# Gate products of the recurrent layers: plain fp32 matmuls replaced by three fp32r passes, and modulation vectors moved between layers

## The chip, the cores and the metric

The kernel runs on one core of one Trainium2 chip, as one launch. The metric is device time in microseconds (us); the profile shows one execution of the same program with a record for every instruction. Five engines matter here: PE (TensorE) multiplies matrices, PEld is the part of PE's queue that loads the stationary operand, DVE (VectorE) and ACT (ScalarE) work on tiles element by element, and SP only issues DMA transfers.

## The reference

One inference step runs two token streams, 128 context tokens and 256 latent tokens (384 columns in the kernel), through four layers of width 1024: a recurrent layer (RG-LRU), a Conformer convolution layer, a neighbourhood-attention layer, and a second recurrent layer. Each layer is a mixer and then an MLP with a squared ReLU, both behind a normalisation that is modulated by six vectors computed from the conditioning (shift, scale and gate for the mixer, and again for the MLP).

```python
h = _modulate(x, sh1, sc1)                       # rmsnorm(x) * (1 + sc1) + sh1
gate_br, rec = jnp.split(h @ w_in, 2, axis=-1)
xf = _dwconv_centred(rec, conv_w, conv_b)        # 4 taps along time
# both directions, blocks of 256 channels:
r  = jax.nn.sigmoid(_block_diag(xf, w_a, b_a))
ig = jax.nn.sigmoid(_block_diag(xf, w_x, b_x))
log_a = -LRU_C * r * jax.nn.softplus(-lam)
a = jnp.exp(log_a)
bx = jnp.sqrt(-jnp.expm1(2.0 * log_a)) * (ig * xf)
h_t = a_t * h_(t-1) + bx_t                       # linear scan
y = (hs_f + hs_b) * gelu(gate_br)
return y @ w_out
```

The products `_block_diag` are the gate products that the change touches. Everything is in fp32.

## The kernel before

**Layout.** Channels lie on the 128 partitions, tokens on the free axis, so a width of 1024 is eight tiles of 128x384. A weight chunk is 128x2048 fp32 (1 MB): two output tiles of eight 128x128 blocks each, or, for the gates, the sixteen 128x128 blocks of one 256-channel block (two directions, two gates, two output tiles, two inputs).

**fp32r with splits.** PE takes fp32r operands, a shorter form of fp32. To keep the precision, the kernel splits each operand into a high and a low part: ACT copies it to an fp32r tile (the high part), and DVE subtracts that from the original (the low part). `mm3` (L452) then issues three matmuls into one PSUM tile: high weight with high input, high weight with low input, low weight with high input. Weights are split when loaded, in `load_chunk` (L196): one DMA into `raw` (two buffers), then for each half an ACT copy at L210 into `whi` and a DVE subtraction at L211 into `wlo` (five buffers each, of half a chunk).

**The gates do otherwise.** A gates chunk is loaded as two 512 KB pieces into `graw` tiles of the layer's own pool (three buffers, L197 to L202), isn't split, and `gates` (L593) multiplies the fp32 tile `xf` with it directly (L605): sixteen fp32 matmuls of 386 columns in each call. The profile shows each of these as two records.

**A recurrent layer** (`lru`, L561) goes through four blocks `b` of 256 channels. `rec(b)` makes the recurrent input, and `conv` (L572) turns it on DVE into `xf` (one multiplication at L584 and three at L587 for each of two tiles). `gates(b)` multiplies, and then ACT computes tanh (L606), exp and tanh (L611, L613), a square (L617) and a square root (L620), while DVE multiplies (L618, L619, L621), scans in both directions (L627, L629), saves the states (L631, L632) and adds the directions (L633). `gbr(b)` computes the gelu branch (L641 to L645), `combine(b)` (L654) multiplies both, and `outs(b)` splits the result (L388, L389) into `yh` and `yl` for the output product `lout`. The tiles `tr` of the gates have two buffers, `ti` and `a` have one, and PSUM tiles for products have six.

**Order.** The order of the calls at the end of `lru` (L715 to L746) and the plan of chunks (`weight_plan`) set the order of the weights; `chunk` (L221) loads one chunk ahead. A scheduler of the language places the instructions of each engine by this order and by when it believes their inputs ready, so a later instruction can stand in front of an earlier one that waits. At run time each engine takes its instructions in the order so fixed. SP issues the weight loads and the modulation loads from one queue.

**Modulation vectors.** There are 192 (four layers, six vectors, eight tiles), made in a fixed order. `pe_mod` makes some on PE; `dve_mod` (L310) makes one on DVE from a 512 KB load, with two multiply-and-accumulate instructions over 1024 columns (L323) and a small addition (L326). `mods(n, pe)` in `lru` does `n` of the one and `pe` of the other in the first layer; the tables `MLPMODS`, `ATTMODS` and the number `VALMODS` (L93 to L98) say how many `dve_mod` follow each step of the MLPs and of the attention layer, and `need` makes those that are still missing.

Of the kernel before, what the change touches and what calls it, by code (L numbers as in the profile page):

```python
# [7 lines left out]
F32 = mybir.dt.float32  # L8
F32R = mybir.dt.float32r
# [5 lines left out]
P = 128  # L15
# [45 lines left out]
def weight_plan():  # L61
    plan = []
    for l in range(DEPTH):
# [11 lines left out]
        for half in range(2):  # L75
# [14 lines left out]
WARM0, WARM1, WARM2 = 20, 8, 4  # L90
RECLAG, PRE1 = 2, 8
WARM3 = (6, 6)
MLPMODS = {(False, 0, 1): (0, 1, 2, 1, 2, 1, 2, 1), (False, 0, 2): (2, 2, 2, 1, 2, 2, 2, 1),  # L93
           (False, 1, 1): (2, 2, 2, 1, 2, 2, 2, 1), (False, 1, 2): (0, 0, 0, 0, 0, 0, 0, 0),
           (True, 0, 1): (0, 1, 1, 1, 1, 2, 2, 0), (True, 0, 2): (0,) * 8,
           (True, 1, 1): (0,) * 8, (True, 1, 2): (0,) * 8}
ATTMODS = (0, 1, 1, 1, 1, 1, 1, 1)
VALMODS = 0  # L98
PTB, BTB = 3, 3
NMOD = DEPTH * 6 * KT  # L100
MODS = []
# [12 lines left out]
def trunk(ctx, tc, wst, wmod, vecs, condr, xin, kcT, vcache, rpbt, diag, ident_in,  # L114
# [33 lines left out]
    def mod_load(i, pool=None, into=None):  # L148
        at = i
        if into is not None:  # L150
            w = into
        elif at < 2 or at in (12, 13) or at > 15:
            w = wp.tile([P, D], F32, tag="pmw", name=f"pmw{i}", bufs=2)
        elif at < 5 or at > 13:
            w = wp.tile([P, D], F32, tag="dmw", name=f"pmw{i}", bufs=3)
        elif at < 9:
            tg, nb = (("tr", 2), ("ti", 1), ("a", 1), ("tr", 2))[at - 5]
            w = pool.tile([P, 4 * LG], F32, tag=tg, name=f"pmw{i}", bufs=nb)[:, :D]
        else:
            w = pool.tile([P, D], F32, tag="graw", name=f"pmw{i}", bufs=3)  # L160
        nc.sync.dma_start(w, wmod[i])
        return w

# [30 lines left out]
    loaded = {}  # L194

    def load_chunk(i):  # L196
        if plan[i][0] == "gates":  # L197
            g = []
            for d in range(2):
                g.append(state["lp"].tile([P, 1024], F32, tag="graw", name=f"graw{i}{d}", bufs=3))  # L200
                nc.sync.dma_start(g[d], wst[i, :, d * 1024:d * 1024 + 1024])
            return g  # L202
        raw = wp.tile([P, 2048], F32, tag="raw", name=f"raw{i}", bufs=2)
        nc.sync.dma_start(raw, wst[i])
        his, los = [], []
        for h in range(2):
            s = slice(h * 1024, h * 1024 + 1024)
            hi = wp.tile([P, 1024], F32R, tag="whi", name=f"whi{i}_{h}", bufs=5)
            lo = wp.tile([P, 1024], F32R, tag="wlo", name=f"wlo{i}_{h}", bufs=5)
            nc.scalar.activation(hi, raw[:, s], AF.Copy)  # L210
            nc.vector.tensor_tensor(lo, raw[:, s], hi.bitcast(F32), op=ALU.subtract)  # L211
            his.append(hi)
            los.append(lo)
        return his, los
# [346 lines left out]
    def lru(l, j, nrm):  # L561
        with tc.tile_pool(name=f"lru{l}", bufs=1) as lp:
# [4 lines left out]
                nc.gpsimd.memset(r, 0.0)  # L567
                recs.append(r)
            nst = lp.tile([P, 2, KT], F32, name=f"nst{l}")
            xfs, gls = {}, {}  # L570

            def conv(b, i, ps, c=None):  # L572
                t = 2 * b + i
                r = recs[t % 2]
                for s, xa, xb in SEG:
                    o = 1 + 2 * s
                    if c is None:
                        nc.scalar.activation(r[:, xa + o:xb + o], ps[:, xa:xb], AF.Copy)
                    else:
                        nc.scalar.activation(r[:, xa + o:xb + o], ps[:, xa:xb], AF.Identity, bias=c[:, s:s + 1])  # L580
                if b not in xfs:
                    xfs[b] = lp.tile([P, 2, LG], F32, tag="xf", name=f"xf{l}{b}", bufs=2)
                xf = xfs[b][:, i]
                nc.vector.tensor_scalar(xf, r[:, 0:LG], lcw[:, j, t, 0:1], lcb[:, j, t:t + 1],  # L584
                                        op0=ALU.mult, op1=ALU.add)
                for k in range(1, 4):
                    nc.vector.scalar_tensor_tensor(xf, r[:, k:k + LG], lcw[:, j, t, k:k + 1], xf,  # L587
                                                   op0=ALU.mult, op1=ALU.add)

            def rec(b):  # L590
                lin([chunk("rec", j, b)], h, f"rec{l}_{b}_", lambda i, ps: conv(b, i, ps))

            def gates(b):  # L593
                cs = chunk("gates", j, b)
                tr = lp.tile([P, 4, LG], F32, tag="tr", name=f"tr{l}{b}", bufs=2)
                ti = lp.tile([P, 4, LG], F32, tag="ti", name=f"ti{l}{b}")
                a = lp.tile([P, 4, LG], F32, tag="a", name=f"a{l}{b}")
# [1 line left out]
                for d in range(2):  # L599
                    for wh in range(2):  # L600
                        for mt in range(2):
                            ps = mm_tile(f"g{l}{b}{d}{wh}{mt}")[:, :LG]
                            for k in range(2):
                                o = ((wh * 2 + mt) * 2 + k) * P
                                matmul(ps, cs[d][:, o:o + P], xf[:, k], start=k == 0, stop=k == 1)  # L605
                            nc.scalar.activation((tr if wh == 0 else ti)[:, d * 2 + mt], ps, AF.Tanh, scale=0.5,  # L606
                                                 bias=hba_[:, wh, j, d, 2 * b + mt:2 * b + mt + 1])
                    for mt in range(2):
                        t = 2 * b + mt
                        i = d * 2 + mt  # L610
                        nc.scalar.activation(a[:, i], tr[:, i], AF.Exp, scale=nch[:, j, d, t:t + 1],  # L611
                                             bias=nch[:, j, d, t:t + 1])
                        nc.scalar.activation(tr[:, i], tr[:, i], AF.Tanh, scale=ch[:, j, d, t:t + 1],  # L613
                                             bias=ch[:, j, d, t:t + 1])
                    s = slice(2 * d, 2 * d + 2)
                    q = lp.tile([P, 2, LG], F32, tag="q", name=f"q{l}{b}{d}")
                    nc.scalar.activation(q, a[:, s], AF.Square)  # L617
                    nc.vector.scalar_tensor_tensor(tr[:, s], q, 1.0, tr[:, s], op0=ALU.add, op1=ALU.mult)  # L618
                    nc.vector.scalar_tensor_tensor(ti[:, s], ti[:, s], 1.0, xf, op0=ALU.add, op1=ALU.mult)  # L619
# [34 lines left out]
                    nc.vector.tensor_tensor(gl[:, :, xa:xb], hs[:, 0:2, a:e_], gl[:, :, xa:xb], op=ALU.mult)  # L654

            def outs(b):
                if b < 3:
                    w_ = lp.tile([P, 1024], F32R, tag="graw", name=f"yh{l}{b}", bufs=3)
                else:
                    w_ = lp.tile([P, 4 * LG], F32R, tag="a", name=f"yh{l}{b}")  # L660
                if b:
# [54 lines left out]
            mods(1)  # L716
            q = gates(0)
            combine(0, q)
            mods(2, 2)
            rec(2)  # L720
            mods(0, 2)
            q1 = gates(1)
            mods(2, 2)
            rec(3)
            mods(0, 2)
            q2 = gates(2)
            mods(2, 2)
            gbr(1)
            mods(0, 2)
            combine(1, q1)  # L730
            q3 = gates(3)
            outs(0)
            outs(1)
            mods(1, 2)
            gbr(2)
            mods(0, 2)
            combine(2, q2)
# [8 lines left out]
            return out_proj(l, "lout", j, y, f"lo{l}")  # L746

    def mlp(l, nrm):
        last = l == DEPTH - 1
        with tc.tile_pool(name=f"mlp{l}", bufs=1) as mp:  # L750
            for half in range(2):
                hid = []
# [17 lines left out]
                while i < 8:  # L770
# [3 lines left out]
                    else:  # L774
                        lin([chunk("ff1", l, half * 8 + i)], h, f"f{l}{half}{i}_", act_)
                        i += 1
                    dve_mod(MLPMODS[last, half, 1][i - 1])
                mv = need(l, G2)
                if half == 1:
                    nx = Norm(l + 1, SC1, SH1)  # L780
                for m in range(KT):
# [5 lines left out]
                    residual(m, ps, G2, mv)  # L787
                    if half == 1:
                        nx.add(m)
                    dve_mod(MLPMODS[last, half, 2][m])  # L790
        return nx

    hb1 = cst.tile([P, 2 * KT], F32, name="hb1")
# [560 lines left out]
```

## Time and profile before

| | us |
|---|---|
| median of 3 runs (1773.96 to 1775.02) | 1774.39 |
| the profiled execution, first to last instruction (its span) | 1769.4 |
| ... of it PE busy | 1741.5 |
| ... DVE busy | 1388.3 |
| ... ACT busy | 939.8 |
| first recurrent mixer, from the first convolution to the last split output | 44 to 168 |
| second recurrent mixer, from the first normalised tile to the last split output | 1349 to 1468 |

The profiled execution has no other time than its span; the median of the runs is 5.0 us longer than that span, which is what lies around the first and the last instruction. The windows of the last two rows are those in which the gates are computed. A window of the profile gives, for each engine, the time in which it had an instruction at work.

### The profile page before, as it was taken

How to read it: one execution, taken by the hardware profiler on the slowest of the kernel's cores; microseconds unless marked ns; L12 is line 12 of the kernel's file. 1: busy time of each engine (PE TensorE's matmuls, PEld its weight loads, DVE VectorE, ACT ScalarE, POOL GpSimd, SP SyncE). 2: the span in 40 equal slices, each digit the busy share in tenths (PEclk: the TensorE clock that was granted, in tenths of full speed). 3: DMA queues.
4: the chain of work that ended last, by engine and by line, in shares of the span. 5: the costliest groups of instructions: out<-in, count | busy, mean ns of one | idle time of the engine just before them, and what ended most of it. 6: DMA issues, size and time to landing. Idle time of an engine off the chain costs nothing.

```text
span 1769.4 us, 27427 instructions
## 1 busy us (share of the span) xinstructions
PE 1741.5 (98%) x10524; PEld 1638.2 (93%) x10524; DVE 1388.3 (78%) x2759; ACT 939.8 (53%) x1691; POOL 21.6 (1%) x46
## 2 busy tenths in 40 slices
PE   8999999999999999999999999999999999999997
PEld 7778999999985999999987889999999789999997
DVE  5998889895697889888576788998997878853443
ACT  4876662453533774254365556624545976733531
POOL 0000000000021000000000000000000000000000
PEclk9999999999999999999999999999999999999999
DMA  9666367663386247765345533676663413543341
GB/s 388 231 215 222 127 222 250 237 248 135 120 240 188 80 151 258 240 242 205 123 171 183 165 112 130 236 250 228 244 242 120 136 67 120 197 148 119 119 135 45
DMA packets 66996, 322.43 MB, mean 182 GB/s; under 512 B 7952, under 2 KB 12176, under 8 KB 43696
## 3 DMA queue, kind: packets, MB, share of 16 engines
q1 hardware_dynamic: 64944, 314.11, 51.5%
q0 software_dynamic: 1920, 6.57, 1.6%
q8 instruction: 82, 1.34, 0.3%
q14 instruction: 50, 0.41, 0.1%
HBM read 316.69 MB, written 3.96 MB: 181 GB/s over the span
## 4 chain that ended last, share of the span: by engine, by line
PE 84%; DVE 8%; ACT 4%; DMA 3%; issue 1%; SPq 0%; POOL 0%; DVEq 0%; ACTq 0%
PE f L125 30%; PE o L125 30%; PE pw L125 4%; PE qk L125 4%; PE lo L125 3%; PE p L125 2%; PE wo L125 2%; PE v L125 2%; PE rec L125 1%; DMA pmw<-wmod 1%; PE cps L125 1%; DVE wlo L211 1%; PE gbr L125 1%; PE po L125 1%; DVE xf L587 1%
## 5 line engine op out<-in xcount | busy, mean ns | idle before, releaser
L210 ACT ACTIVATE whi<-raw 128x1024 fp32r<-128x1024 f32 x360 | 378.0, 1058 | 557.8 <-PE o L125 337.8
L211 DVE TENSOR_TENSOR wlo<-raw,whi 128x1024 fp32r<-128x1024 f32 x360 | 437.8, 1220 | 166.5 <-ACT whi L210 166.4
L323 DVE SCALAR_TENSOR_TENSOR mjunk<-dmw,condb 128x1024 bf16<-128x1024 f32 x300 | 365.2, 1217 | 1.3
L125 PE MATMUL o<-hl,whi 128*128 128x384 f32 x1024 | 343.0, 335 | 0.0
L125 PE MATMUL o<-hh,wlo 128*128 128x384 f32 x1024 | 343.0, 335 | 0.0
L125 PE MATMUL o<-hh,whi 128*128 128x384 f32 x1024 | 343.0, 335 | 0.0
L125 PEld LDWEIGHTS o<-hh,wlo 128*128 128x128 f32 x1024 | 192.2, 188 | 0.0
L125 PEld LDWEIGHTS o<-hh,whi 128*128 128x128 f32 x1024 | 192.2, 188 | 0.0
L125 PEld LDWEIGHTS o<-hl,whi 128*128 128x128 f32 x1024 | 192.2, 188 | 0.0
L480 DVE SCALAR_TENSOR_TENSOR x<-o,modv,x 128x128 f32<-128x128 f32 (+1 forms) x128 | 47.4, 412 | 87.8 <-PE o L125 87.6
L125 PE MATMUL g<-xf,graw 128*128 128x386 f32 x256 | 87.3, 497 | 1.9 <-DVE gl L645 1.9
L125 PEld LDWEIGHTS g<-xf,graw 128*128 128x128 f32 x256 | 48.7, 192 | 35.4 <-DVE gl L645 2.6
L766 DVE TENSOR_TENSOR hl<-s,hh 128x384 fp32r<-128x384 f32 x128 | 70.9, 554 | 13.4 <-ACT s L765 8.7
L764 ACT ACTIVATE hh<-r 128x384 fp32r<-128x384 f32 x128 | 67.1, 524 | 3.5
L765 ACT ACTIVATE s<-r 128x384 f32<-128x384 f32 x128 | 65.1, 509 | 0.0
L760 ACT ACTIVATE r<-f 128x384 f32<-128x384 f32 x112 | 53.2, 475 | 7.8 <-PE f L125 7.8
L125 PE MATMUL lo<-yh,wlo 128*128 128x384 f32 x128 | 43.3, 338 | 0.1
L125 PE MATMUL lo<-yh,whi 128*128 128x384 f32 x128 | 43.3, 340 | 0.0
L125 PE MATMUL lo<-yl,whi 128*128 128x384 f32 x128 | 43.0, 336 | 0.0
L125 PE MATMUL cps<-z,dg 128*32 128x399 f32 (+2 forms) x448 | 34.7, 468 | 3.9 <-DMA z<-zd 3.9
L876 DVE SCALAR_TENSOR_TENSOR zt<-zp,vec,zt 128x399 f32<-128x399 f32 x58 | 36.7, 632 | 1.2
L125 PEld LDWEIGHTS cps<-z,dg 128*32 128x32 f32 x448 | 15.1, 114 | 22.7 <-issue 21.5
(1510 smaller groups left out, 4041.2 us busy)
## 6 DMA issues: line engine op xcount, KB each, us to landing
raw<-wst SPq DMA_DIRECT2D x180, 1024.0 KB, 5.0
dmw<-wmod SPq DMA_DIRECT2D x150, 512.0 KB, 4.2
pmw<-wmod SPq DMA_DIRECT2D x38, 512.0 KB, 6.5
graw<-wst SPq DMA_DIRECT2D x16, 512.0 KB, 5.6
bt<-rpbt SPq DMA_DIRECT2D x16, 384.0 KB, 3.8
z<-zd POOLq DMA_DIRECT2D x24, 213.5 KB, 6.5
dg<-diag SPq DMA_DIRECT2D x6, 512.0 KB, 4.2
pmwl<-wmod SPq DMA_DIRECT2D x4, 512.0 KB, 6.8
```

The source lines that it names most:

```text
L125: i = nc.tensor.matmul(*a, **kw)
L210: nc.scalar.activation(hi, raw[:, s], AF.Copy)
L211: nc.vector.tensor_tensor(lo, raw[:, s], hi.bitcast(F32), op=ALU.subtract)
L323: nc.vector.scalar_tensor_tensor(mjunk, w, 0.5, condb[:, s], op0=ALU.mult, op1=ALU.mult, accum_out=mod_tile(l)[:, c, m, s:s + 1]))
L480: nc.vector.scalar_tensor_tensor(x[m][:, xa:xb], ps[:, a:b], mv[:, g, m, s:s + 1], x[m][:, xa:xb], op0=ALU.mult, op1=ALU.add)
L587: nc.vector.scalar_tensor_tensor(xf, r[:, k:k + LG], lcw[:, j, t, k:k + 1], xf, op0=ALU.mult, op1=ALU.add)
L760: nc.scalar.activation(r, ps[:, :N], AF.Relu)
L764: nc.scalar.activation(hh, r, AF.Square)
L765: nc.scalar.activation(s, r, AF.Square)
L766: nc.vector.tensor_tensor(hl, s, hh.bitcast(F32), op=ALU.subtract)
L876: nc.vector.scalar_tensor_tensor(t, z[:, k:k + CG], dww[:, m, k:k + 1], t, op0=ALU.mult, op1=ALU.add)
```

## The change

- `load_chunk` loses its branch for the gates. A gates chunk is now loaded like any other: one 1 MB DMA into `raw`, two ACT copies into `whi`, two DVE subtractions into `wlo`.
- `conv` splits each `xf` tile as soon as it is made, into `xh` (ACT) and `xl` (DVE), new tiles with two buffers each. `xf` itself stays, since L619 reads it.
- `gates` issues `mm3` in place of one fp32 matmul: 48 fp32r matmuls of 386 columns in each call in place of 16 fp32 ones.
- The pool `graw` is gone. The `yh` tiles of `outs` for b = 0, 1, 2 now lie in `xh`, `xh` and `xl`, and the loads of modulation vectors 9, 10 and 11 go to buffers of `whi`, `wlo` and `dmw`.
- The numbers of `dve_mod` change. By the calls, four leave the mixer of the first layer (three of `mods(2, 2)` become `mods(1, 2)`, one `mods(1, 2)` becomes `mods(0, 2)`; the short title says six). Two of them go to the first half of the first MLP, two to the start of the attention layer (`VALMODS`), and the attention's last step makes one that `need` made there before. `MLPMODS` now has an entry for each layer.

```diff
-MLPMODS = {(False, 0, 1): (0, 1, 2, 1, 2, 1, 2, 1), (False, 0, 2): (2, 2, 2, 1, 2, 2, 2, 1),
...
-ATTMODS = (0, 1, 1, 1, 1, 1, 1, 1)
-VALMODS = 0
+MLPMODS = [((0, 1, 2, 1, 2, 2, 2, 2), (2, 2, 2, 1, 2, 2, 2, 1), (2, 2, 2, 1, 2, 2, 2, 1), (0,) * 8),
+           ((0, 1, 2, 1, 2, 1, 2, 1), (2, 2, 2, 1, 2, 2, 2, 1), (2, 2, 2, 1, 2, 2, 2, 1), (0,) * 8),
...
+ATTMODS = (0, 1, 1, 1, 1, 1, 1, 2)
+VALMODS = 2
...
-            w = pool.tile([P, D], F32, tag="graw", name=f"pmw{i}", bufs=3)
+            tg, nb = (("whi", 5), ("wlo", 5), ("dmw", 3))[at - 9]
+            w = wp.tile([P, D], F32, tag=tg, name=f"pmw{i}", bufs=nb)
...
-        if plan[i][0] == "gates":
-            g = []
-            for d in range(2):
-                g.append(state["lp"].tile([P, 1024], F32, tag="graw", name=f"graw{i}{d}", bufs=3))
-                nc.sync.dma_start(g[d], wst[i, :, d * 1024:d * 1024 + 1024])
-            return g
...
+                    xss[b] = (lp.tile([P, 2, LG], F32R, tag="xh", name=f"xh{l}{b}", bufs=2),
+                              lp.tile([P, 2, LG], F32R, tag="xl", name=f"xl{l}{b}", bufs=2))
...
+                split(xf, xss[b][0][:, i], xss[b][1][:, i])
...
-                cs = chunk("gates", j, b)
+                whs, wls = chunk("gates", j, b)
+                xh, xl = xss[b]
...
-                                matmul(ps, cs[d][:, o:o + P], xf[:, k], start=k == 0, stop=k == 1)
+                                mm3(ps, whs[d][:, o:o + P], wls[d][:, o:o + P], (xh[:, k], xl[:, k]), k == 0, k == 1)
...
-                if b < 3:
-                    w_ = lp.tile([P, 1024], F32R, tag="graw", name=f"yh{l}{b}", bufs=3)
+                if b < 2:
+                    w_ = lp.tile([P, 2 * LG], F32R, tag="xh", name=f"yh{l}{b}", bufs=2)
+                elif b == 2:
+                    w_ = lp.tile([P, 2 * LG], F32R, tag="xl", name=f"yh{l}{b}", bufs=2)
...
-            mods(2, 2)
+            mods(1, 2)
             rec(2)
             mods(0, 2)
             q1 = gates(1)
-            mods(2, 2)
+            mods(1, 2)
             rec(3)
             mods(0, 2)
             q2 = gates(2)
-            mods(2, 2)
+            mods(1, 2)
             gbr(1)
...
             outs(1)
-            mods(1, 2)
+            mods(0, 2)
             gbr(2)
...
-                    dve_mod(MLPMODS[last, half, 1][i - 1])
+                    dve_mod(MLPMODS[l][2 * half][i - 1])
```

More of the change, by code (lines that the diff above doesn't have):

```diff
@@ L92 @@
 WARM3 = (6, 6)
-MLPMODS = {(False, 0, 1): (0, 1, 2, 1, 2, 1, 2, 1), (False, 0, 2): (2, 2, 2, 1, 2, 2, 2, 1),
-           (False, 1, 1): (2, 2, 2, 1, 2, 2, 2, 1), (False, 1, 2): (0, 0, 0, 0, 0, 0, 0, 0),
-           (True, 0, 1): (0, 1, 1, 1, 1, 2, 2, 0), (True, 0, 2): (0,) * 8,
-           (True, 1, 1): (0,) * 8, (True, 1, 2): (0,) * 8}
-ATTMODS = (0, 1, 1, 1, 1, 1, 1, 1)
-VALMODS = 0
+MLPMODS = [((0, 1, 2, 1, 2, 2, 2, 2), (2, 2, 2, 1, 2, 2, 2, 1), (2, 2, 2, 1, 2, 2, 2, 1), (0,) * 8),
+           ((0, 1, 2, 1, 2, 1, 2, 1), (2, 2, 2, 1, 2, 2, 2, 1), (2, 2, 2, 1, 2, 2, 2, 1), (0,) * 8),
+           ((0, 1, 2, 1, 2, 1, 2, 1), (2, 2, 2, 1, 2, 2, 2, 1), (2, 2, 2, 1, 2, 2, 2, 1), (0,) * 8),
+           ((0, 1, 1, 1, 1, 2, 2, 0), (0,) * 8, (0,) * 8, (0,) * 8)]
+ATTMODS = (0, 1, 1, 1, 1, 1, 1, 2)
+VALMODS = 2
 PTB, BTB = 3, 3
@@ L569, in lru @@
             nst = lp.tile([P, 2, KT], F32, name=f"nst{l}")
-            xfs, gls = {}, {}
+            xfs, xss, gls = {}, {}, {}
             def conv(b, i, ps, c=None):
@@ L748, in mlp @@
     def mlp(l, nrm):
-        last = l == DEPTH - 1
         with tc.tile_pool(name=f"mlp{l}", bufs=1) as mp:
@@ L789, in mlp @@
                         nx.add(m)
-                    dve_mod(MLPMODS[last, half, 2][m])
+                    dve_mod(MLPMODS[l][2 * half + 1][m])
         return nx
```

## The prediction

> **What bounds the kernel now.** I read first the page's head, then its chain that ended last.
>
> ```profile
> span 1769.4 us, 27427 instructions
> PE 1741.5 (98%) x10524; PEld 1638.2 (93%) x10524; DVE 1388.3 (78%) x2759; ACT 939.8 (53%) x1691; POOL 21.6 (1%) x46
> PE 84%; DVE 8%; ACT 4%; DMA 3%; issue 1%; SPq 0%; POOL 0%; DVEq 0%; ACTq 0%
> ```
>
> PE fills 98% of the span, so whatever shortens PE's work seems to shorten the kernel. But shares are averages over stages, and the change touches only the two recurrent mixers. So next I asked for the busy time by windows: the two mixers from the first convolution to the last split output, then one turn of each (from the start of one block's gates to the start of the next block's).
>
> ```profile
> core 0: us, PE busy (x) PEld busy (x) DVE busy (x) ACT busy (x) POOL busy (x), PEclk, DMA share, GB/s
> 44.00:168.00 124.00, 121.47 (x836) 97.89 (x835) 115.58 (x231) 94.01 (x161) 0.00 (x0) 1.00 0.65 224
> 1349.00:1468.00 119.00, 116.97 (x548) 98.08 (x547) 101.91 (x184) 95.75 (x158) 0.00 (x0) 0.99 0.29 93
> 78.81:100.48 21.67, 21.67 (x152) 16.33 (x148) 21.67 (x39) 18.08 (x29) 0.00 (x0) 1.00 0.68 210
> 1385.69:1404.47 18.78, 18.78 (x81) 14.47 (x81) 17.23 (x29) 17.30 (x28) 0.00 (x0) 1.00 0.33 112
> ```
>
> Here PE isn't alone. In the first mixer DVE works 115.58 of 124 us and is idle 8.4; in its turn both engines are full. In the second DVE is idle 17.1 of 119, and in its turn PE is full with DVE and ACT at 92%. Any gain of PE has to pass two engines with little room, and the change gives both more to do.
>
> The end of the window matters, since there PE waits for y:
>
> ```profile
> 1466.20 1.03 DVE L389 TENSOR_TENSOR yl<-gl,yh 128x384 fp32r<-128x384 f32 x2 [0.59 <-ACT yh L388]
> 1467.10 0.34 PE L125 MATMUL lo<-yl,whi 128*128 128x384 f32 x1
> ```
>
> DVE ends the last split at 1467.2 and PE reads a low part at 1467.1, in the same us. If DVE ends later, PE stands still; if PE comes earlier, it waits. So the mixer's time is that of the later of the two.
>
> **PE's part.** The price of a gates call and of 48 fp32r passes, from the timeline of PE:
>
> ```profile
> 1358.55 0.34 PE L125 MATMUL gbr<-h310h,whi 128*128 128x384 f32 x1
> 1366.93 0.49 PE L125 MATMUL g<-xf,graw 128*128 128x386 f32 x1
> 1385.69 10.56 PE L125 MATMUL g<-xf,graw 128*128 128x386 f32 x32
> 1395.79 0.64 PE L125 MATMUL rec<-h310h,whi 128*128 128x384 f32 x1
> ```
>
> The 48 passes of a gbr chunk take 1366.93 - 1358.55 = 8.38 us. A gates call (32 records) and the 48 passes behind it take the turn's 18.78; with two calls of 48 passes it would be 16.76. That is 2.0 us less for each call, 16 us for eight. If PE alone set the pace, the span would fall by 16.
>
> A rule of the Trainium skill ("Perfetto Trace Analysis", section Identifying the Most-Contended Engine) judges PE by the busy time of its weight loads, not of its matmuls. The loads' records here are 188 ns, so 48 passes would need 9.0 us by it and the gain would be 11 us instead of 16; the measured 8.38 decides, and the forecast below uses neither.
>
> **DVE's and ACT's part.** The operations that are added have rows of their own kind:
>
> ```profile
> L210 ACT ACTIVATE whi<-raw 128x1024 fp32r<-128x1024 f32 x360 | 378.0, 1058 | 557.8 <-PE o L125 337.8
> L211 DVE TENSOR_TENSOR wlo<-raw,whi 128x1024 fp32r<-128x1024 f32 x360 | 437.8, 1220 | 166.5 <-ACT whi L210 166.4
> L323 DVE SCALAR_TENSOR_TENSOR mjunk<-dmw,condb 128x1024 bf16<-128x1024 f32 x300 | 365.2, 1217 | 1.3
> ...
> L388 ACT ACTIVATE yh<-gl 128x384 fp32r<-128x384 f32 x8 | 3.8, 521 | 6.7 <-DVE gl L654 6.7
> 1372.16 2.35 DVE L211 TENSOR_TENSOR wlo<-raw,whi 128x1024 fp32r<-128x1024 f32 x2
> 160.14 1.02 DVE L389 TENSOR_TENSOR yl<-gl,yh 128x384 fp32r<-128x384 f32 x2
> ```
>
> Back to back, two weight subtractions take 2.35 us, so one more costs DVE 1.14 (their ends overlap); two 384-column subtractions take 1.02, so one more costs 0.47. Each mixer gets eight of the first (four gates chunks, two halves) and eight of the second (four blocks, two tiles): 9.1 + 3.8 = 12.9 us of DVE. ACT gets eight copies of at most 1.05 and eight of at most 0.52: 12.6 us.
>
> In the first mixer four modulation vectors leave. One is two instructions of group L323: 365.2 / 150 = 2.43 us, so 9.7 us of DVE go. Net, DVE gets 12.9 - 9.7 = 3.2 us in the first mixer and 12.9 in the second, where there is nothing to take out: 16.1 us together. By turns: in the second mixer DVE comes to 17.23 + 2 x 1.14 + 2 x 0.47 = 20.5 and ACT to 17.30 + 3.1 = 20.4, against PE's 16.8 and the 18.78 that a turn takes today. In the first, DVE comes to 21.67 + 3.2 - 2.4 = 22.5 against PE's 19.7 and today's 21.67. Both mixers become DVE's, and both turns longer.
>
> How much longer depends on how much of DVE's idle time the added work fills. That time, 8.4 + 17.1 = 25.5 us, is waiting for ACT:
>
> ```profile
> DVE tr L618 <- ACT q L617: 7.8, 4, 4.3
> DVE ti L621 <- ACT tr L620: 6.4, 4, 1.7
> ...
> ACT a L611 <- DVE nst L631: 2.7, 2, 1.4
> ACT ti L606 <- DVE nst L631: 2.6, 1, 2.6
> ACT tr L606 <- DVE gl L654: 2.9, 1, 2.9
> ...
> PE g L125 <- DVE gl L645: 1.9, 1, 1.9
> ```
>
> (All of the second mixer.) DVE waits for ACT's square and square root of the same block, while ACT waits for DVE's scans to free `a`, `ti` and `tr`; weight splits can stand in the first kind of gap, but no split shortens the chain. So some idle time stays. I take 8.4 us for each mixer: that is what the first mixer keeps today with DVE and PE both nearly full. Then the first takes 115.58 + 3.2 + 8.4 = 127.2 (+3.2) and the second 101.91 + 12.9 + 8.4 = 123.2 (+4.2): **+7.4 us**. Bounds: idle time filled to nothing gives 16.1 - 25.5 = -9.4; none of it filled gives +16.1.
>
> **The small edits.** The four vectors land in the first MLP and in the attention layer:
>
> ```profile
> 200.00:330.00 130.00, 130.00 (x748) 130.00 (x747) 119.32 (x222) 61.75 (x100) 0.00 (x0) 1.00 0.65 219
> 900.00:945.00 45.00, 45.00 (x223) 34.75 (x223) 31.31 (x81) 27.16 (x52) 0.00 (x0) 1.00 0.42 147
> ```
> ```profile
> PE pmp L125 <- DMA pmw<-wmod: 0.3, 1, 0.3
> ```
>
> Each place gets two, 4.9 us of DVE, into 10.7 and 13.7 us of DVE's idle time with PE full, and two loads of 512 KB, where the DMA engines are busy 0.65 and 0.42 of the time: nothing. Without that cover it would be up to 4.9 in the first place. Gates chunks now pass `raw` and its two buffers: the same bytes, and DVE's subtraction must be done before SP can issue the load two chunks on, with the modulation loads queued behind it; PE waited 0.3 us in all for those loads in the first mixer (the last row), so I take 0, with up to 2. The first pass of a gates call now waits for one more copy and one more subtraction behind the last tap of the convolution, 0.52 + 0.55 us (1.02 less 0.47); where PE has just been fed, that is hidden behind the 8.38 us of the product in front of it, and where DVE is late it is in the sum above. A copy L210 for a gates chunk stands in ACT's queue and waits for a weight buffer; behind it stand the tanhs (L606) that empty PSUM for PE: part of the ACT coupling, and of the upper bound. Vectors 9 to 11 and `yh` only change buffers: 0; the first gbr chunk must now wait for a buffer of the first rec chunk, at most one copy and one subtraction, 2.3 us.
>
> **Sum.** Against the profiled execution 1769.4 + 7.4 = 1776.8; the median is 5.0 us above that span, so 1774.4 + 7.4 = 1781.8. A measurement of this kernel can tell about 0.2% (3.5 us) from no change.
>
> **Rivals.**
> 1. *The idle time is filled (faster).* With DVE behind, its queue always holds a ready split, and PE runs ahead with later products. All 25.5 us filled give 1774.4 - 9.4 = 1765.0. It decides once DVE keeps less than 25.5 - 16.1 = 9.4 us idle in both mixers. For it: the turn of the first mixer shows no idle time at all. Against: the block chain above. Chance 0.14.
> 2. *The full gain of PE arrives,* 1774.4 - 16 = 1758.4. DVE's work would have to leave the windows: 118.8 and 114.8 us don't fit into 116 and 111. Chance 0.07.
> 3. *Fill and load balance.* Idle time falls to about 9.4, the kernel stays within 3.5 us of 1774.4; also where the change wouldn't do what it says, three passes costing what fp32 costs. Chance 0.23.
> 4. *Nothing is filled,* since ACT (94.01 and 95.75 plus 12.6) is as tight as DVE: 1774.4 + 16.1 = 1790.5. It decides if the second mixer's 17.1 us of idle time stays. Chance 0.12.
> 5. *The clock falls.* PE will wait in each turn. One such wait is in the trace:
>
> ```profile
> 1423.23:1437.23 14.00, 12.05 (x33) 6.60 (x33) 12.07 (x19) 7.64 (x13) 0.00 (x0) 0.88 0.23 75
> ```
>
> Behind the 1.9 us wait the granted clock of 14 us is 0.88, 1.7 us lost. In each of eight calls, and on the chain, that is 13.4 us on top of the forecast: 1795. Mostly it would hide, as PE has 3 us of room in a turn. The Trainium skill ("TensorE: Matmul & The Clock Gate", Part 1) has the clock at half after an idle window of about 3.4 us; the trace shows a fall after less. Chance 0.04.
>
> **How the numbers follow.** The forecast itself (+3.5 to +12) has 0.40. Slower by over 0.2%: 0.40 + 0.12 + 0.04 = 0.56; same 0.23; faster 0.14 + 0.07 = 0.21. The likeliest case's own range is 1778 to 1786. The range reaches from the filled case less 1 to the unfilled case plus the small edits' 2: 1764 to 1792.
>
> **What would show it.** Right: in the windows from the first `xf` to the last `yl`, DVE busy about 119 and 115 us with around 8 idle, PE busy falling to some 113 and 109 with waits "PE g <- DVE" or PE waiting for `xl`; the second mixer's turn 20.5 or more; g in x48 passes with some 8.4 us from first to last where nothing stops it; MLPs and attention unchanged. Wrong: a turn of the second mixer under 18.8, DVE idle under 9 us in both mixers together, or a change of over 3 us outside the two mixers.

## The result, and the profile after

The changed kernel takes 1783.38 us (median of 4 runs, 1781.84 to 1785.01) against 1774.70 for the kernel before beside it (4 runs): a ratio of 1.0051, 95% interval 1.0038 to 1.0065. It is slower by 8.7 us; the forecast was 1781.8. (The times below are medians of 4 to 12 executions, that of before_again is a single one; one of the ten of copies_back took 6991 us and is not in its ratio.)

The head of the page after has almost the same shares as before:

```profile
span 1780.1 us, 27727 instructions
PE 1736.6 (98%) x10652; PEld 1667.0 (94%) x10652; DVE 1413.0 (79%) x2793; ACT 961.7 (54%) x1723; POOL 21.6 (1%) x46
```

PE's busy time fell by 4.9 us where sixteen were to be saved, and DVE's rose by 24.7. The profiled execution took 1780.1 us, 10.7 more than that of before. A run's time is only 1.7 us above its span (this one counts as 1781.84), so the 5.0 us between median and span of before, which the prediction took for what lies around the execution, were mostly scatter between executions. The profile of before was some 3 us quicker than its kernel's median, and this one 1.5; so the stages below add up to more than the 8.7 us between the medians.

Where did the 10.7 us come from? The first product of each normalisation is a border between two stages. From the timeline of PE, before and then after:

```profile
196.54 0.81 PE L125 MATMUL n_4p<-n_4a,ones 128*128 128x384 f32 x2
465.20 0.81 PE L125 MATMUL n_1p<-n_1a,ones 128*128 128x384 f32 x2
620.33 0.81 PE L125 MATMUL n_4p<-n_4a,ones 128*128 128x384 f32 x2
888.99 0.81 PE L125 MATMUL n_1p<-n_1a,ones 128*128 128x384 f32 x2
1075.80 0.81 PE L125 MATMUL n_4p<-n_4a,ones 128*128 128x384 f32 x2
1344.46 0.81 PE L125 MATMUL n_1p<-n_1a,ones 128*128 128x384 f32 x2
1492.56 0.81 PE L125 MATMUL n_4p<-n_4a,ones 128*128 128x384 f32 x2
```
```profile
202.34 0.81 PE L125 MATMUL n_4p<-n_4a,ones 128*128 128x384 f32 x2
470.99 0.81 PE L125 MATMUL n_1p<-n_1a,ones 128*128 128x384 f32 x2
619.94 0.81 PE L125 MATMUL n_4p<-n_4a,ones 128*128 128x384 f32 x2
888.59 0.81 PE L125 MATMUL n_1p<-n_1a,ones 128*128 128x384 f32 x2
1077.19 0.81 PE L125 MATMUL n_4p<-n_4a,ones 128*128 128x384 f32 x2
1345.85 0.81 PE L125 MATMUL n_1p<-n_1a,ones 128*128 128x384 f32 x2
1503.13 0.81 PE L125 MATMUL n_4p<-n_4a,ones 128*128 128x384 f32 x2
```

Differences of neighbouring rows are the stages. The first one is cut once more, at the product of the prologue's last vectors (`pmp14r`, at 41.94 before and 45.33 after):

| stage | before | after | change | forecast |
|---|---|---|---|---|
| prologue, to 41.94 and 45.33 | 41.9 | 45.3 | +3.4 | 0, up to 2 |
| first mixer behind it | 154.6 | 157.0 | +2.4 | +3.2 |
| first MLP | 268.7 | 268.7 | 0 | 0 |
| Conformer | 155.1 | 149.0 | -6.2 | 0 |
| attention (second MLP in front: 0) | 186.8 | 188.6 | +1.8 | 0 |
| second recurrent mixer (third MLP in front: 0) | 148.1 | 157.3 | +9.2 | +4.2 |

Behind it nothing changes. The sum is +10.6. So the two mixers lost more than forecast, and 6 us came back in a layer that the change doesn't touch.

The windows that the prediction named, after. The columns are those of before: length, the busy times of PE, PEld, DVE, ACT and POOL with their counts, and the granted clock PEclk. The first two are the mixers; that of the first starts 2.1 us behind the prologue's end, as it did before, which is some 5 us ahead of the first `xf` (49.1 before, 52.1 after). The last two run from the start of one block's gates to the next block's:

```profile
47.39:174.20 126.81, 118.20 (x903) 110.60 (x901) 117.75 (x224) 104.32 (x178) 0.00 (x0) 0.97 0.55 200
1350.40:1479.00 128.60, 116.77 (x614) 115.35 (x613) 114.89 (x200) 106.61 (x174) 0.00 (x0) 0.92 0.29 99
81.65:108.25 26.60, 23.05 (x169) 21.53 (x165) 24.65 (x42) 21.86 (x38) 0.00 (x0) 0.87 0.47 178
1391.16:1413.98 22.82, 20.00 (x98) 19.68 (x97) 21.11 (x33) 21.05 (x34) 0.00 (x0) 0.85 0.30 98
```

DVE is busy 117.75 and 114.89 us, as forecast (118.8 and 114.8). Its idle time is 9.1 and 13.7 us, where 8.4 each was forecast. The second mixer's turn is 22.8 us against 18.8, with DVE and ACT both at 21.1. PE's busy time did not fall to 109 in the second mixer: the granted clock is 0.92 there, and 109 us of work at 0.99 would be 117 at 0.92 (an estimate). What PE waits for, from the waits after:

```profile
PE g L125 <- DVE gl L644: 6.8, 2, 6.0
PE pmp L125 <- DMA pmw<-wmod: 6.6, 3, 3.6
PE g L125 <- DVE wlo L206: 4.4, 2, 3.1
PE rec L125 <- DVE wlo L206: 3.7, 2, 2.8
```

Before, PE's matmuls waited 1.9 us for `gl` and 0.7 for `wlo`. Now PE waits for low parts of weights (`wlo`) and for DVE to empty a PSUM tile of the gelu branch (`gl`). On DVE's timeline the `gl` of the longest wait stands behind the four scans of a block, and the two `wlo` of the second mixer behind convolution steps of a later block.

### The profile page after: what moved, and what is told of

Read it like the earlier page. It is cut to its first block, busy times and chain, and to the rows that moved or that the text cites. A ratio compares the mean times of both kernels' runs of the same rounds, so it can differ in the third digit from the quotient of the medians.

```text
span 1780.1 us, 27727 instructions
## 1 busy us (share of the span) xinstructions
PE 1736.6 (98%) x10652; PEld 1667.0 (94%) x10652; DVE 1413.0 (79%) x2793; ACT 961.7 (54%) x1723; POOL 21.6 (1%) x46
## 4 chain that ended last, share of the span: by engine, by line
PE 85%; DVE 7%; ACT 4%; DMA 2%; issue 1%; SPq 0%; POOL 0%; DVEq 0%; ACTq 0%
PE f L125 30%; PE o L125 30%; PE pw L125 4%; PE lo L125 4%; PE qk L125 4%; PE p L125 2%; PE wo L125 2%; PE v L125 2%; PE rec L125 1%; PE g L125 1%; PE cps L125 1%; PE gbr L125 1%; PE po L125 1%; DMA pmw<-wmod 1%; DVE xf L584 1%; DMA raw<-wst 1%
## 5 line engine op out<-in xcount | busy, mean ns | idle before, releaser
L205 ACT ACTIVATE whi<-raw 128x1024 fp32r<-128x1024 f32 x376 | 394.2, 1059 | 560.1 <-PE o L125 328.3
L206 DVE TENSOR_TENSOR wlo<-raw,whi 128x1024 fp32r<-128x1024 f32 x376 | 457.4, 1222 | 162.8 <-ACT whi L205 162.2
L766 DVE TENSOR_TENSOR hl<-s,hh 128x384 fp32r<-128x384 f32 x128 | 71.1, 556 | 11.6 <-ACT s L765 7.4
L125 PE MATMUL g<-xh,whi 128*128 128x386 f32 x128 | 46.0, 360 | 6.8 <-DVE gl L644 6.8
L125 PE MATMUL g<-xh,wlo 128*128 128x386 f32 x128 | 44.4, 361 | 4.4 <-DVE wlo L206 4.4
L125 PE MATMUL g<-xl,whi 128*128 128x386 f32 x128 | 45.6, 356 | 0.0
```

Source lines behind the costliest of these rows:

```text
L125: i = nc.tensor.matmul(*a, **kw)
L766: nc.vector.tensor_tensor(hl, s, hh.bitcast(F32), op=ALU.subtract)
```

## The experiments

A table of stages for all profiles stands first, because most verdicts are read from it. Taken as above, in us; the time is the median in rounds with the kernel before.

| kernel | time | ratio, 95% interval | prologue | first mixer behind it | Conformer | attention | second mixer |
|---|---|---|---|---|---|---|---|
| before | 1773.8 | | 41.9 | 154.6 | 155.1 | 186.8 | 148.1 |
| before_again | 1772.4, one run | | 44.2 | 154.6 | 155.0 | 186.3 | 147.7 |
| after | 1783.4 | 1.0038 to 1.0065 | 45.3 | 157.0 | 149.0 | 188.6 | 157.3 |
| vectors_only | 1771.6 | 0.9978 to 1.0010 | 42.1 | 154.0 | 154.9 | 188.1 | 148.7 |
| passes_only | 1790.8 | 1.0082 to 1.0115 | 43.9 | 165.0 | 150.4 | 186.6 | 156.6 |
| no_low_parts | 1774.0 | 0.9994 to 1.0012 | 46.8 | 149.6 | 150.0 | 189.0 | 155.1 |
| pool_low | 1792.7 | 1.0096 to 1.0133 | 46.3 | 165.4 | 151.1 | 188.4 | 162.8 |
| two_passes | 1788.5 | 1.0065 to 1.0136 | 43.4 | 158.9 | 153.2 | 188.7 | 158.0 |
| passes_free2 | 1758.4 | 0.9896 to 0.9926 | 42.7 | 146.7 | 149.2 | 188.6 | 146.3 |
| copies_back | 1769.6 | 0.9966 to 0.9992 | 41.7 | 150.8 | 150.9 | 189.0 | 151.2 |
| subs_back | 1774.3 | 0.9995 to 1.0019 | 42.0 | 153.6 | 150.5 | 188.2 | 154.5 |
| first_only | 1775.2 | 0.9992 to 1.0024 | 45.3 | 157.0 | 148.8 | 188.0 | 148.2 |
| first_pe | 1772.0 | 0.9980 to 1.0008 | 45.8 | 152.2 | 152.2 | 188.2 | 148.3 |
| first_pe_buf | 1771.5 | 0.9975 to 0.9995 | 45.2 | 153.7 | 151.9 | 189.5 | 147.6 |

The kernel before was run anew with each group (medians 1773.5 to 1774.7); the ratios are to those. A stage whose work is the same in two kernels can still differ, since the scheduler orders each program anew: the first mixer of first_pe and of first_pe_buf by 1.5 us, the prologue of before and before_again, which are one program, by 2.3. A single difference of 1 to 2 us shows little by itself.

### First question: is it DVE?

The theory of the forecast: DVE's added subtractions lengthen both mixers. The rivals: ACT's copies do it, or the clock. The first five kernels take the change apart.

**no_low_parts**: the changed kernel without DVE's added work. It leaves out the low parts of the gates' operands.

```diff
-            nc.vector.tensor_tensor(lo, raw[:, s], hi.bitcast(F32), op=ALU.subtract)
+            if plan[i][0] != "gates":
+                nc.vector.tensor_tensor(lo, raw[:, s], hi.bitcast(F32), op=ALU.subtract)
...
-                split(xf, xss[b][0][:, i], xss[b][1][:, i])
+                nc.scalar.activation(xss[b][0][:, i], xf, AF.Copy)
```

> The changed kernel without DVE's low parts for the gates: the weight subtractions of the gates chunks and the subtractions for xl are left out, and the passes multiply the high parts three times (the low parts of the gate products are missing from the result). PE's 48 passes, ACT's copies and the loads stay. Theory (DVE's added work sets the two mixers): 12.9 us of DVE leave each mixer, both fall under the time before, the whole to 1757 to 1766. Rival (ACT's added copies set them): the second mixer stays at least 6 us longer than before, the whole at 1777 or more. Rival (the clock, falling after waits, makes the loss): PE still waits for the high parts, the whole between 1768 and 1777.

It took 1774.04 us: 9.3 of the time went, but not the 17 to 26 that the theory asked for. The table says where: the first mixer fell by 7.4, to 149.6; the second by 2.2 only and stayed 7.0 above before. There something else holds it. The stage fits the rival of ACT's copies (at least 6 us longer), the total fits the rival of the clock (1768 to 1777); the second question below goes into both.

**vectors_only** and **passes_only**: the two halves of the change, each alone. The first is the kernel before with the new tables and calls of `dve_mod`; the second is the changed kernel with the old ones.

> The kernel before with only the new places of the modulation vectors (four less in the first mixer, two more in the first MLP, two more at the start of the attention layer). Theory: PE was full in the first mixer, so freeing 9.7 us of DVE gives it little: 1771 to 1775. The shorter Conformer layer of the changed kernel (6 us less than before) should show here if the moved vectors make it: then 1767 to 1770. Attention should be about 2 us longer.

> The changed kernel with the modulation vectors where they were before. Theory (DVE sets the first mixer): 9.7 us of DVE come back there, the first mixer gets 6 to 10 us longer than in the changed kernel, the second keeps its +9: the whole at 1787 to 1794. Rival (ACT or the clock sets it, DVE has room): 1782 to 1786.

Moving the vectors alone changes nothing that can be measured (1771.55; the interval has 1 in it), and it leaves the Conformer at 154.9. With the passes in, their leaving is worth 165.0 - 157.0 = 8.0 us in the first mixer, as the theory expected, of the 9.7 us of DVE that the prediction counted for them. They cost the attention stage 1.2 to 3.2 us: 188.0 to 189.5 in all kernels with the moved vectors, 186.3 to 186.8 in those without. In the first MLP, with 10.7 us of DVE idle in 130, they cost nothing, as forecast.

**pool_low**: the gates' weight subtractions on GpSimd instead of DVE.

```diff
-            nc.vector.tensor_tensor(lo, raw[:, s], hi.bitcast(F32), op=ALU.subtract)
+            (nc.gpsimd if plan[i][0] == "gates" else nc.vector).tensor_tensor(lo, raw[:, s], hi.bitcast(F32), op=ALU.subtract)
```

> The changed kernel with the low parts of the gates chunks subtracted on GpSimd in place of DVE: 9.1 us of DVE leave each mixer, nothing is left out of the result. Theory (DVE's load): 1766 to 1776, if a subtraction on GpSimd ends before PE needs it. Rival (the chain from the load over both parts to PE sets the start of each gates call): a slower subtraction makes PE wait longer, 1783 or more.

1792.67 us, slower than the changed kernel. The group of these subtractions, from the groups of instructions (count, busy time, mean ns of one, idle time before):

```profile
L206 POOL TENSOR_TENSOR wlo<-raw,whi 128x1024 fp32r<-128x1024 f32 x16 | 42.5, 2673 | 191.4 <-ACT whi L205 106.5 <-DVE xf L584 53.5 <-PE rec L125 16.8
```

One takes 2.67 us there, against 1.22 on DVE. And DVE got nothing for it: in the second mixer it has eight instructions less than after (249 and 257) and is busy as long (139.3 and 140.4 us). The timeline of DVE shows why, in the moment when GpSimd works on such a half from 1386.63 to 1388.99:

```profile
1387.01 2.41 DVE L384 TENSOR_TENSOR xl<-xf,xh 128x386 fp32r<-128x386 f32 x1 [1.80 <-ACT xh L383]
1389.34 0.61 DVE L584 SCALAR_TENSOR_TENSOR xf<-rec,vec,xf 128x386 f32<-128x386 f32 x1
```

A subtraction that takes 0.55 us elsewhere took 2.41 and ended 0.43 us after GpSimd's. This kernel is therefore no test of DVE's theory: the work was moved, but DVE kept the time.

**two_passes**: all splits of the changed kernel, but two passes in each product.

```diff
-                                mm3(ps, whs[d][:, o:o + P], wls[d][:, o:o + P], (xh[:, k], xl[:, k]), k == 0, k == 1)
+                                matmul(ps, whs[d][:, o:o + P], xh[:, k], start=k == 0, stop=False)
+                                matmul(ps, wls[d][:, o:o + P], xl[:, k], start=False, stop=k == 1)
```

> The changed kernel with all its splits, but two of the three passes in each gates product (high by high and low by low; it leaves out the two cross terms' larger half, and one pass in three): 16 passes less in each call, 16 x 0.175 = 2.8 us of PE, 22 us for eight calls. If DVE's and ACT's queues set the mixers' time, PE's work doesn't matter: 1780 to 1786, as changed. If PE is still on the path (its passes, or the clock), 1763 to 1774.

With a third of the passes gone the kernel took 1788.48 us, over all that was expected; the mixers' stages are 1.9 and 0.7 us longer. PE's busy time in them did fall, by 5.5 and 8.1 us (to 142.9 and 137.4), not by the 22 us of passes at full pace. So PE's work does not set the pace of the changed kernel in either mixer. PE has more to wait for, and the mean clock of the profile falls to 0.982 (after: 0.989, before: 0.995).

### Second question: what is PE's gain worth, and what does each engine take of it?

**passes_free2**: three passes, no split. (passes_free, the same idea with the unsplit tiles read as fp32r where they lie, left no time to report.) The last tap of the convolution rounds `xf` as it writes it, and the weights are rounded ones that are there already, those of the chunk in front; the low parts are left out.

```diff
+                prev = loaded[state["w"] - 1][0]
                 cs = chunk("gates", j, b)
...
-                                matmul(ps, cs[d][:, o:o + P], xf[:, k], start=k == 0, stop=k == 1)
+                                for t_ in range(3):
+                                    matmul(ps, prev[d][:, o:o + P], xf[:, k],
+                                           start=k == 0 and t_ == 0, stop=k == 1 and t_ == 2)
```

> The kernel before with the six vectors moved, and three fp32r passes for each fp32 product of the gates, with no split: the last tap of the convolution rounds xf as it writes it, and the weights are the high halves of the chunk in front (so the gates are computed from other weights and without low parts; the gates' own chunks are still loaded). DVE and ACT get nothing. If the added splits (DVE's subtractions and ACT's copies) ate PE's gain, both mixers fall: by 4 to 8 us the second, against 148.5, and as much the first, against 196; the time is 1756 to 1764. If PE's gain is not to be had in these mixers (the block chain from tanh to scan sets the turn, or the clock falls), the second stays at 147 or more and the time at 1768 or more.

1758.36 us. PE's gain exists: 13.2 us under vectors_only. But the stages place it otherwise than expected. The first mixer falls by 7.3 us (forecast for PE alone: 8); the second by 2.4 only; 5.6 are the Conformer's. In the second mixer PE no longer fills the stage even with nothing added: its window has DVE idle for 18.5 us and PE for 6.1 (below), 4.1 of them in one wait for DVE's `gl` and 1.9 in one for ACT's `ti`. So the chain of a block, in which DVE and ACT work by turns, sets the pace there as much as PE's work does.

**copies_back** and **subs_back** add to this kernel one engine's share of the splits, in place: on the gates' chunks, which nobody reads, and on `xf`, for which PE waits:

```diff
                 nc.sync.dma_start(g[d], wst[i, :, d * 1024:d * 1024 + 1024])
+                nc.scalar.activation(g[d], g[d], AF.Copy)
...
+                nc.scalar.activation(xr, xr.bitcast(F32), AF.Copy)
```
```diff
                 nc.sync.dma_start(g[d], wst[i, :, d * 1024:d * 1024 + 1024])
+                nc.vector.tensor_tensor(g[d], g[d], g[d], op=ALU.subtract)
...
+                nc.vector.tensor_tensor(xr, xr.bitcast(F32), xr.bitcast(F32), op=ALU.max)
```

> The three passes without splits, and ACT's 32 added copies put back as in-place copies: two of 1024 columns for each gates chunk, which nobody reads, and one of 386 for each xf, for which PE waits. (As there, the gates are computed from other weights, without low parts.) DVE gets nothing, and the gates' chunks keep their own buffers. If ACT's time is what held the kernel with passes and without DVE's low parts, its stages come back: the second mixer at 153 to 156 us (turns near 21 us, against 18.3 and 19.6 without the copies), the first 2 to 4 us longer behind the prologue than 146.7, the time 1766 to 1773. If the shared buffers of raw, whi and wlo were its cause, the second mixer stays at 146 to 149 and the time at 1757 to 1763.

> The three passes without splits, and DVE's 32 added operations put back in place: two of 1024 columns for each gates chunk, unread, and one of 386 for each xf (its maximum with itself). ACT gets nothing. (As there, the gates are computed from other weights, without low parts.) If each engine's work costs by itself, DVE's costs what it cost on top of the copies: some 7 us in the first mixer (154 behind the prologue) and 2 to 3 in the second (148 to 149), 1766 to 1769. If DVE bounds both mixers, as the forecast had it, the second goes to 152 or more and the time to 1771 or more. If it costs only together with ACT's copies, 1758 to 1762.

1769.55 and 1774.28 us: ACT's copies alone cost 11.2, DVE's subtractions alone 15.9, both with the real buffers and low parts (after) 25.0. The second mixer's window from border to border, for before, passes_free2, copies_back, subs_back, no_low_parts and after:

```profile
1344.46:1492.56 148.10, 146.07 (x709) 126.65 (x709) 127.57 (x241) 115.85 (x199) 0.00 (x0) 0.99 0.32 106
```
```profile
1333.10:1479.43 146.33, 140.26 (x773) 138.36 (x773) 127.84 (x241) 115.09 (x199) 0.00 (x0) 0.97 0.32 107
```
```profile
1338.38:1489.59 151.21, 140.50 (x774) 137.03 (x773) 127.88 (x241) 125.70 (x215) 0.00 (x0) 0.98 0.31 103
```
```profile
1340.29:1494.78 154.49, 142.24 (x774) 137.93 (x773) 139.49 (x257) 114.46 (x199) 0.00 (x0) 0.97 0.29 100
```
```profile
1341.33:1496.46 155.13, 143.47 (x773) 139.73 (x773) 127.46 (x241) 126.17 (x215) 0.00 (x0) 0.96 0.30 103
```
```profile
1345.85:1503.13 157.28, 145.45 (x774) 143.50 (x774) 140.38 (x257) 126.58 (x215) 0.00 (x0) 0.93 0.31 102
```

The busy times stand in the order PE, PEld, DVE, ACT. ACT gets 10.6 us and the stage 4.9; DVE gets 11.7 and the stage 8.2; both, 10.95. (The first mixer alike: 9.9 us of ACT cost 4.1, 12.0 of DVE 7.0.) In the four windows with copies or subtractions no engine is full, yet nearly half of ACT's added time and seven tenths of DVE's arrive. The likely reading is that the engines wait for each other along the block chain, and that what is added to either lies in that chain. A falling clock is not needed for it: these two stages grow at a clock of 0.98 and 0.97, where passes_free2 has 0.97. For the subtractions the numbers of "DVE bounds both mixers" fit (the stage over 152, the time over 1771), but a mixer that DVE alone bounds would not have grown by the copies. Neither of the two expectations for the copies fits whole: the stage with copies alone (151.2) is in between, and no_low_parts, which has the same ACT time, is 3.9 us longer. What it has besides is the shared `raw`, `whi` and `wlo` buffers and a PE that waits for the gates' own copies; which of these makes the 3.9 us was not separated.

### Third question: can the rest be had?

**first_only** keeps the passes in the first mixer and gives the second its fp32 gates and `graw` back.

```diff
+        if plan[i][0] == "gates" and plan[i][1] == 1:
+            g = []
...
+                                if j:
+                                    matmul(ps, whs[d][:, o:o + P], xf[:, k], start=k == 0, stop=k == 1)
+                                else:
+                                    mm3(ps, whs[d][:, o:o + P], wls[d][:, o:o + P], (xh[:, k], xl[:, k]), k == 0, k == 1)
```

> The changed kernel in the first mixer and for the vectors; the second mixer with fp32 gates as before. By the stage borders the second mixer lost 9.2 us: 1783.4 - 9.2 = 1774 (1772 to 1777), its stage back at 148 us. The Conformer's 6 us less: if it comes with the first mixer's passes, it stays (stage at 149 to 151 us); if it belongs to the second mixer's buffers or to the execution, it may be 155 again.

1775.16 us: the second mixer's stage is 148.2 again, and the other stages are those of the changed kernel. The second mixer's loss is local.

**first_pe** goes on from there: three of the four vectors left on DVE in the first mixer go to PE.

```diff
-            mods(1, 2)
+            mods(0, 3)
             rec(2)
```

(The same at two other calls.)

> As the kernel with passes in the first mixer only, and three of the four modulation vectors that DVE still makes there go to PE (a pair costs PE 1.08 us; one costs DVE 2.43): DVE gets 7.3 us less, PE 1.6 more and three more loads of 512 KB through the two buffers of pmw. If DVE bounds the first mixer (four vectors out were worth 6.7 us there with the passes in), it falls by another 3 to 6 us: 1768 to 1772. If the loads of the vectors bind (PE waited 6.6 us for them in the changed kernel), no gain or a loss: 1774 to 1780.

1771.97 us. The first mixer falls to 152.2, by 4.8 us for 7.3 us of DVE's work: again about two thirds. That is 2.4 under before, the first configuration with real splits whose first mixer is shorter than before; seven vectors fewer on DVE are part of that, and the same with fp32 gates was not run. In first_pe_buf, with the same work there, the stage is 153.7, so these 4.8 us are uncertain by 1.5. **first_pe_buf** was to take back the prologue's loss as well:

```diff
-            tg, nb = (("whi", 5), ("wlo", 5), ("dmw", 3))[at - 9]
-            w = wp.tile([P, D], F32, tag=tg, name=f"pmw{i}", bufs=nb)
+            tg, nb = (("whi", 5), ("wlo", 5), ("q", 1))[at - 9]
+            w = (pool if tg == "q" else wp).tile([P, D], F32, tag=tg, name=f"pmw{i}", bufs=nb)
```

> As the kernel with passes in the first mixer only and three vectors more on PE, but vector 11 of the prologue is loaded into the buffer of q in place of the third buffer of dmw, so that its load needn't wait for a vector product of PE. If that wait, with SP's queue behind it, made the first vectors late (PE waited 2.7 us for pmw), the wait falls below 0.8, the first stage by 2 to 3.5 us from 197.95, and the time is 1768 to 1770. If the wait comes from the order of the loads on full DMA queues, nothing changes: 1772.

It didn't: PE still waits 2.8 us for `pmw`, and the prologue is 45.2, so the buffer of vector 11 is not what makes the wait. The time, 1771.52, has a ratio of 0.9985 (0.9975 to 0.9995): the best kernel with passes and real splits, and still within the 0.2% that can't be told from no change.

**before_again** is a second profile of the kernel before.

> The kernel before, word for word, with a second profile. If the length of the Conformer's stage (155.1 us before, 148.8 to 154.9 in the others, with the same work) is a matter of the execution, it may come out anywhere from 149 to 155 here; if it belongs to the kernel before, 155. All other stages within 1.5 us of the first profile.

The Conformer's stage is 155.0 again, so its length belongs to the kernel, not to the execution. The row in which most of the difference arises, on PE's timeline, for before, before_again and after (in brackets the wait and what ended it):

```profile
563.85 5.35 PE L125 MATMUL cps<-z,dg 128*32 128x256 f32 x64 [3.94 <-DMA z<-zd]
```
```profile
566.05 5.27 PE L125 MATMUL cps<-z,dg 128*32 128x256 f32 x64 [3.84 <-DMA z<-zd]
```
```profile
566.76 3.66 PE L125 MATMUL cps<-z,dg 128*32 128x256 f32 x64 [0.81 <-DMA z<-zd]
```

PE waits 3.9 us for a load and then does the same 64 products in 5.35 us instead of 3.66: 3.1 + 1.7 = 4.8 of the 6.2 us. In all eleven kernels with fp32r gates in the first mixer the stage is 149 to 153, in the others 155. That the new order of the program moved the load is the likely reason; it was not shown.

## Why the prediction was right, and where it was wrong

**Right: PE's 98% promised nothing.** A gates call takes 48 passes of 0.178 us (1391.16 to 1399.72, 8.56 us; forecast 8.4), so PE's 16 us are real on paper; without splits 9.7 of them arrive in the mixers (passes_free2), with them none.

**Right: DVE's work and the first mixer.** Added and removed operations took about what their rows said: busy times within 1.1 us of the forecast, and +2.4 for the first mixer where +3.2 was forecast. (A vector costs DVE 2.75 us and not 2.43: the sum left out the two accumulator reads and the small addition of each, 1.3 us for four.) From the prologue's end to the border, before and after:

```profile
41.94:196.54 154.60, 152.07 (x1012) 128.50 (x1011) 140.54 (x288) 114.10 (x203) 0.00 (x0) 1.00 0.63 219
```
```profile
45.33:202.34 157.01, 148.40 (x1076) 140.80 (x1076) 143.14 (x285) 124.65 (x219) 0.00 (x0) 0.98 0.56 201
```

DVE's busy time grew by 2.6, the stage by 2.4: its idle time, 14.1 and 13.9 us, was not filled at all.

**Wrong in size: the second mixer, +9.2 instead of +4.2.** The step was "I take 8.4 us for each mixer", carried over from the first mixer's idle time. In the second 13.7 us stayed, and those 5.3 us are the whole error. The first mixer's idle time was no measure for the second. Rival 4 (nothing is filled) was nearer to this mixer than the forecast: 17.1 us of idle time became 13.7. The prediction named ACT and gave its 12.6 us no price in the sum; copies_back shows the copies alone costing 4.9 us in this stage. But they are not the whole reason. subs_back adds nothing on ACT, and its stage is 154.5 all the same, 6.4 above before, with 15.0 us of DVE idle (border to border: before 20.5, after 16.9). By this count the forecast would have left 11.8 us, so over half of what it missed stays without any added copy. The remaining 2.8 us up to after come with the copies, the shared buffers, the real low parts and a clock of 0.93, and were not taken apart.

**Wrong: two small edits at nothing.** The prologue lost 3.4 us against the first profile of before, over the bound of 2 for its loads, and 1.1 against the second. PE's timeline, before and after, for the pair of vectors 8 and 9:

```profile
27.33 1.07 PE L125 MATMUL pmp<-pmw,condp 128*32 128x128 f32 x28 [0.40 <-DMA pmw<-wmod]
```
```profile
30.29 1.69 PE L125 MATMUL pmp<-pmw,condp 128*32 128x128 f32 x28 [3.58 <-DMA pmw<-wmod]
```

In the six profiles of kernels that load vectors 9 to 11 into `graw` this product starts at 27.3 to 29.2 us, in the eight others at 29.7 to 30.9, and the prologue lasts 42.4 us on average against 45.2. So a loss of some 2.8 us goes with the buffers of the change, but a single pair of profiles can't show it: before_again (44.2) has a longer prologue than two kernels with the new buffers (43.4 and 43.9). Which buffer it is, first_pe_buf didn't find. The vectors moved to the attention layer cost 1.2 to 3.2 us in spite of 13.7 idle us of DVE in 45. After, PE waits there 1.4 us for DVE's `pe`, which it did not before; that this is the whole way of the loss was not shown.

**Wrong: "a change of over 3 us outside the two mixers" was to disprove the forecast.** The Conformer's -6.2 is one against either profile of before, the prologue's +3.4 only against the first. With the attention they sum to -1.0, so the total came out well partly by luck: mixers +11.6 (forecast +7.4), the rest -1.0 (forecast 0).

**The clock (rival 5) fell, and its price is open.** PE's clock fell in both mixers (0.97 and 0.92) and ate its saving in busy time (116.77 in the second window instead of 109). two_passes shows that PE's work is hidden there even so: less of it gained nothing. copies_back and subs_back show that the second mixer grows without a lower clock. What the lower clock costs by itself was not measured; the 13.4 us that rival 5 put on top did not come.

## What to carry to other kernels

Price a change of the form "fewer matmul passes for more splitting" as a trade between engines: here PE's 16 us were worth 10 in the mixers, and some 25 us of DVE with 23 of ACT cost 25 of time (1783.4 - 1758.4), with idle time on both in the window. Where engines alternate along a chain, idle time of one is not room: here four to seven tenths of what was added arrived, and that holds for the engine that you didn't count, too. Compare stages by their borders before the total: errors of 5 and 6 us hid behind a median that was 1.6 off. And take a second profile of the kernel before, so that you know which stage differences are scatter.

## What the runs showed of the hardware

**The same wait had different consequences for the clock.** In the changed kernel, PE's timeline behind a wait of 3.05 us:

```profile
1372.95 0.69 PE L125 MATMUL g<-xh,wlo 128*128 128x386 f32 x1 [3.05 <-DVE wlo L206]
1373.44 0.53 PE L125 MATMUL g<-xh,whi 128*128 128x386 f32 x1
1373.76 0.53 PE L125 MATMUL g<-xl,whi 128*128 128x386 f32 x1
...
1378.88 0.34 PE L125 MATMUL g<-xh,wlo 128*128 128x386 f32 x1
1379.06 0.34 PE L125 MATMUL g<-xh,whi 128*128 128x386 f32 x1
```

The passes go at 0.32 us each until 1378.9 and at 0.18 from there: 5.9 us at half pace. In passes_only the same wait of the same length:

```profile
1378.95 0.44 PE L125 MATMUL g<-xh,wlo 128*128 128x386 f32 x1 [3.05 <-DVE wlo L206]
1379.23 0.34 PE L125 MATMUL g<-xh,whi 128*128 128x386 f32 x1
...
1380.23 0.52 PE L125 MATMUL g<-xl,whi 128*128 128x386 f32 x1
1380.56 0.85 PE L125 MATMUL g<-xh,wlo 128*128 128x386 f32 x2
...
1383.42 0.34 PE L125 MATMUL g<-xh,whi 128*128 128x386 f32 x1
```

Here PE starts again at full pace, slows only at 1380.2, and is back at 1383.4: 3.2 us. The Trainium skill ("TensorE: Matmul & The Clock Gate", Part 1) says that the gate watches a free-running window of about 3.4 us, which doesn't start with the work; that the same wait costs one stretch of 3.2 us here and nearly two there agrees with it. Its other statement, that it takes an idle window of that length, does not hold here: in no_low_parts passes went at 0.32 us each behind a wait of 1.99 us. Nor does the length of a wait alone decide. The same fp32 product, in before and in vectors_only:

```profile
1430.54 7.16 PE L125 MATMUL g<-xf,graw 128*128 128x386 f32 x16 [1.95 <-DVE gl L645]
```
```profile
1431.68 5.47 PE L125 MATMUL g<-xf,graw 128*128 128x386 f32 x16 [2.55 <-DVE gl L645]
```

Behind the shorter wait it took 7.16 us, behind the longer one 5.47. So the 1.7 us that rival 5 read off the first of these rows is not the price of every such wait.

**GpSimd held DVE up.** Beside the row above, the four products of `ti` and `tr` in pool_low's second mixer, by the groups of its instructions, and the same after:

```profile
L620 DVE TENSOR_TENSOR ti<-ti,tr 128x1544 f32<-128x1544 f32 x4 | 9.3, 2320 | 11.4 <-ACT tr L619 11.4
```
```profile
L620 DVE TENSOR_TENSOR ti<-ti,tr 128x1544 f32<-128x1544 f32 x4 | 7.1, 1767 | 5.2 <-ACT tr L619 5.2
```

The two long ones of the four (3.06 and 2.68 us) started while GpSimd subtracted, the other two (1.77) did not, and the subtraction of 386 columns above took 2.41 us instead of 0.55. The Trainium skill ("SBUF — State Buffer", section SBUF: two separate sides) says that the two share a pair of ports which whoever starts first holds for a whole instruction; these rows agree with it.
